# Narrow experts of a mixture of experts: left and right column products pinned in turns, and their middle columns turned by transpositions

## The chip, the core and the metric

One core of one Trainium2 chip runs the whole program once. The metric is the device time of that execution in microseconds (us), lower is better. Times are medians of the runs named.

## What is computed

A two-layer encoder on 256 tokens plus 16 learned ones, model width 1024, all float32. The change lies in the last part of layer 1, the top-2-of-8 SwiGLU experts with hidden width 3584:

```python
def swiglu(x, w_gate, w_up, w_down):
    return (jax.nn.silu(x @ w_gate) * (x @ w_up)) @ w_down

def moe_swiglu(x, w_router, b_router, w_gate, w_up, w_down):
    ...
    y = jnp.zeros(x.shape, jnp.float32)
    for e in range(N_EXPERTS):
        y = y + gates[..., e:e + 1] * swiglu(x, w_gate[e], w_up[e], w_down[e]).astype(jnp.float32)
    return y.astype(x.dtype)
```

Attention, the dense SwiGLU of layer 0, the RWKV mixer of layer 1 and the layer norms come before it or after it and are not touched.

## The kernel before

The experts are ordered by how many tokens chose them, and stand in the places `KINDS = 'WNWWNWWN'`. A wide place (W) has room for 128 tokens, a narrow one (N) for 64; there are five wide and three narrow ones. Each expert is worked in two tiles of `FT` = 1792 hidden columns, so the loop `for n in range(16)` in `moe` goes over 16 tiles. Tile n computes its gate and up products, while the hidden columns of tile n-1 are turned (put with the hidden index on the partitions) and multiplied with the down matrix. So three kinds of step share TensorE at any time: gate and up of this tile, turning of the last, down of the last. After an expert's second tile, `combine` (L1508, L1510) adds its result to the sum `ymoe`.

A wide tile takes every weight piece apart into two rounded halves, `w_hi` (ScalarE, L124) and `w_lo` (VectorE or GpSimd, L127), and makes three products of each (L1414 for gate and up, L134 to L136 for down). A narrow tile uses the raw float32 weights. Its 64 tokens fill only half of TensorE's 128 columns, so there are two products that stand beside each other: in `stream_narrow` (L1429) h = 0 is the gate product on the left 64 columns and h = 1 the up product on the right 64; in `down_narrow` (L1478) q = 0 and q = 1 are the left and right half of the output width. A float32 product shows as two records in the trace.

Turning is done in `hidden_narrow`: two steps for each tile, each of seven products with the identity (L1459, 64 rows by 128 strided hidden columns as the stationary operand, 64 identity columns moving), and a VectorE copy out of PSUM (L1460). `pt` and `hth` have one buffer each, so a step also waits for the copy before it. In wide tiles the same is done with transpositions (L1445). `hid`, the tile that is turned, is made by a SiLU on ScalarE (L1616) and a product on VectorE (L1618).

Weights come by SP's DMA queue (L1545), 896 KB each, into a ring of 17 buffers, in program order.

The order of instructions on each engine is not the order of the code: a scheduler sets it, by its own estimate of when each instruction is ready and by the dependences. `tc.keep_in_program_order(ins)` adds a dependence of issue order alone: `ins` comes behind the instruction that was traced just before it on its engine. Columns that an instruction uses, left or right, are part of the built program, not of the trace.

Of the kernel before, what the change touches and what calls it, by code (L numbers as in the profile page):

```python
# [17 lines left out]
NF = 8  # L18
# [8 lines left out]
FT = 1792  # L27
NB = FT // 128
# [66 lines left out]
class Trunk:  # L95
# [15 lines left out]
    def load(self, src, r0, kt, c0, nc_, pitch):  # L111

        raw = next(self.raws)()[:, :kt * nc_].rearrange("p (k c) -> p k c", k=kt)
        self.nc.sync.dma_start(raw, self.row_ap(src, r0 * pitch + c0, [[pitch, 128], [128 * pitch, kt], [1, nc_]]))
        return raw
# [1304 lines left out]
    def stream_narrow(self, psum, xs, load, steps):  # L1420

        ps = [psum.tile([128, 2, 512], F32, name="pgu", bufs=2) for _ in range(2)]
        for k in range(NF):
            raws = [load(kind, k) for kind in range(2)]
            for a in range(2):
                for b in range(2):
                    o = 896 * a + 448 * b
                    for h in range(2):
                        self.nc.tensor.matmul(ps[a][64 * h:64 * h + 64, b, :448], xs[:, k, :], raws[h][:, o:o + 448], start=k == 0,  # L1429
                                              stop=k == NF - 1)  # L1430
                for f in steps.pop(2 * k + a, ()):
                    f()
        return ps
# [17 lines left out]
    def hidden_narrow(self, mp, psum, s, H):  # L1451
        nc = self.nc

        def step(i0):
            if i0 == 0:
                H['h'] = mp.tile([128, NB, 64], F32, name="hth", bufs=1)
            pt = psum.tile([128, 7, 64], F32, name="pt", bufs=1)
            for j in range(7):
                nc.tensor.matmul(pt[:, j, :], s[64:128, i0 + j:FT:NB], self.ident[64:128, 64:128], start=True, stop=True)  # L1459
            nc.vector.tensor_copy(H['h'][:, i0:i0 + 7, :], pt)  # L1460

        return [lambda i=i: step(i) for i in (0, 7)]
# [11 lines left out]
    def down_narrow(self, h, load, pd, half, first, last):  # L1474
        for j in range(4 * half, 4 * half + 4):
            raw = load(j)
            for o, n, i, q, c in self.pieces(j, 0, FT):
                self.nc.tensor.matmul(pd[64 * q:64 * q + 64, c:c + n], h[:, i, :], raw[:, o:o + n], start=first and i == 0,  # L1478
                                      stop=last and i == NB - 1)

    @staticmethod
    def pieces(j, a, b):
# [253 lines left out]
```

## Time and profile before

| | us |
|---|---|
| median of 3 runs | 1922.72 (1917.08 to 1924.86) |
| the profiled execution, its own time | 1925.96 |
| its span, first to last instruction | 1923.9 |
| TensorE (PE) busy | 1764.4 (92%) |
| VectorE (DVE) busy | 1279.4 (66%) |
| ScalarE (ACT) busy | 913.4 (47%) |
| GpSimd (POOL) busy | 625.4 (33%) |
| mean granted TensorE clock | 0.934 of full speed |

Busy time is a union, so products that overlap are counted once. The experts take the stretch from about 900 us to 1906 us of the span; the first narrow tile's products start at 1000.7 us. The three narrow experts work at about 1000 to 1135, 1384 to 1515 and 1770 to 1900 us, with wide ones between. The granted clock has two levels, 2.4 GHz (1.00 in a stretch) and 1.2 GHz (0.50).

### The profile page before, as it was taken

The numbers are of one execution on the slowest core, as the hardware profiler recorded it, in microseconds if no ns is written. First come the engines' busy times: TensorE is split into PE (matmuls) and PEld (weight loads), VectorE is DVE, ScalarE is ACT, GpSimd is POOL, SyncE is SP. The second block draws the span as 40 slices with busy tenths as digits, with TensorE's granted clock in tenths as the row PEclk, the third lists the DMA queues.
The fourth block names the chain that finished last, engine by engine and source line by source line (L and its number), as shares of the span: only waits on it lengthen the run. The fifth ranks groups of instructions, "written<-read, shape, count | busy, mean of one in ns | idle before, by whom it ended". The sixth has DMA issues, their size and how long they took to land. (4 is left out here: it accounts for less than half of the span.)

```text
span 1923.9 us, 30672 instructions
## 1 busy us (share of the span) xinstructions
PE 1764.4 (92%) x11506; PEld 1406.3 (73%) x11506; DVE 1279.4 (66%) x2135; ACT 913.4 (47%) x1612; POOL 625.4 (33%) x551
## 2 busy tenths in 40 slices
PE   6997999978988878897999999999999999999995
PEld 6887999966666666777876577888765678887642
DVE  6886655587678786836884247999732478897412
ACT  4675444364254434434763135777531356765300
POOL 4333100256545544303542013544310134444201
PEclk9999999988788878888999999999999999999988
DMA  6331555521200000536699899989998999889980
GB/s 209 103 111 45 175 176 187 178 64 46 77 24 29 23 23 23 220 119 257 236 333 403 347 382 341 351 325 330 332 362 329 374 360 342 320 321 336 404 336 25
DMA packets 130737, 431.79 MB, mean 224 GB/s; under 512 B 13689, under 2 KB 78674, under 8 KB 130578
## 3 DMA queue, kind: packets, MB, share of 16 engines
q1 hardware_dynamic: 127202, 427.78, 60.4%
q10 hardware_dynamic: 3376, 1.95, 0.4%
q8 instruction: 92, 1.51, 0.3%
q14 instruction: 67, 0.55, 0.1%
HBM read 428.66 MB, written 1.05 MB: 223 GB/s over the span
## 5 line engine op out<-in xcount | busy, mean ns | idle before, releaser
L127 DVE TENSOR_TENSOR w_lo<-w_raw,w_hi 128x896 fp32r<-128x896 f32 (+2 forms) x445 | 648.9, 1498 | 163.0 <-ACT w_hi L124 159.1
L124 ACT CAST w_hi<-w_raw 128x896 fp32r<-128x896 f32 (+2 forms) x580 | 537.9, 960 | 271.6 <-PE pgu L1414 65.9
L127 POOL TENSOR_TENSOR w_lo<-w_raw,w_hi 128x1024 fp32r<-128x1024 f32 (+1 forms) x135 | 335.9, 2489 | 673.2 <-ACT w_hi L124 525.4
L1414 PE MATMUL pgu<-w_hi,xe 128*128 128x448 f32 x1280 | 305.2, 373 | 2.4 <-DVE hid L1610 1.6
L1414 PEld LDWEIGHTS pgu<-w_hi,xe 128*128 128x128 f32 x1280 | 240.2, 190 | 27.0 <-issue 5.1
L1429 PE MATMUL pgu<-w_raw,xs 128*64 128x448 f32 x768 | 173.7, 559 | 0.0
L1414 PE MATMUL pgu<-w_lo,xe 128*128 128x448 f32 x640 | 167.4, 371 | 5.4 <-DVE w_lo L127 5.3
L1414 PEld LDWEIGHTS pgu<-w_lo,xe 128*128 128x128 f32 x640 | 118.7, 189 | 22.4 <-DVE w_lo L127 8.9
L1429 PEld LDWEIGHTS pgu<-w_raw,xs 128*64 128x64 f32 x768 | 65.2, 140 | 87.6 <-issue 85.6
L135 PE MATMUL pd<-w_lo,hth 128*128 128x512 f32 (+1 forms) x320 | 121.7, 385 | 6.2 <-DVE w_lo L127 4.5
L136 PE MATMUL pd<-w_hi,htl 128*128 128x512 f32 (+1 forms) x320 | 119.5, 375 | 0.0
L134 PE MATMUL pd<-w_hi,hth 128*128 128x512 f32 (+1 forms) x320 | 100.4, 374 | 4.1 <-ACT w_hi L124 4.1
L1478 PE MATMUL pdn<-w_raw,hth 128*64 128x512 f32 (+1 forms) x384 | 85.5, 568 | 0.0
L135 PEld LDWEIGHTS pd<-w_lo,hth 128*128 128x128 f32 x320 | 62.0, 194 | 27.8 <-POOL w_lo L127 6.5
L134 PEld LDWEIGHTS pd<-w_hi,hth 128*128 128x128 f32 x320 | 58.5, 194 | 17.7 <-ACT w_hi L124 5.7
L134 PE MATMUL pj<-xh,w_hi 128*128 128x272 f32 x192 | 59.3, 309 | 11.7 <-ACT w_hi L124 4.7
L136 PEld LDWEIGHTS pd<-w_hi,htl 128*128 128x128 f32 x320 | 62.0, 194 | 9.1
L1478 PEld LDWEIGHTS pdn<-w_raw,hth 128*64 128x64 f32 x384 | 34.7, 143 | 39.5 <-issue 33.8
L136 PE MATMUL pj<-xh,w_lo 128*128 128x272 f32 x192 | 57.5, 300 | 0.6 <-DVE w_lo L127 0.6
L135 PE MATMUL pj<-xl,w_hi 128*128 128x272 f32 x192 | 57.3, 298 | 0.0
L1618 DVE TENSOR_TENSOR hid<-hid,pgu 64x896 f32<-64x896 f32 x12 | 12.9, 1091 | 61.1 <-ACT hid L1616 61.1
L139 DVE TENSOR_TENSOR htl<-pt,hth 128x512 fp32r<-128x512 f32 (+1 forms) x40 | 24.6, 616 | 41.3 <-ACT hth L139 41.3
(634 smaller groups left out, 3620.5 us busy)
## 6 DMA issues: line engine op xcount, KB each, us to landing
w_raw<-in_moe_w_down_dram SPq DMA_DIRECT2D x128, 896.0 KB, 7.1
w_raw<-in_moe_w_gate_dram SPq DMA_DIRECT2D x126, 896.0 KB, 7.0
w_raw<-in_moe_w_up_dram SPq DMA_DIRECT2D x126, 896.0 KB, 7.0
w_raw<-in_attn_w_in_dram SPq DMA_DIRECT2D x12, 1024.0 KB, 9.1
w_raw<-in_rw_w_rkv_dram SPq DMA_DIRECT2D x12, 1024.0 KB, 5.0
w_raw<-in_ffn_w_gate_dram SPq DMA_DIRECT2D x11, 1024.0 KB, 7.6
w_raw<-in_ffn_w_up_dram SPq DMA_DIRECT2D x11, 1024.0 KB, 5.1
w_raw<-in_ffn_w_down_dram SPq DMA_DIRECT2D x8, 1024.0 KB, 5.0
```

Of the source, the lines that this page charges most:

```text
L124: nc.scalar.copy(hi, raw)
L127: self.parted = eng.tensor_tensor(lo, raw, hi.bitcast(F32), op=OP.subtract)
L134: mm(ps, wh, xh, start=start, stop=False)
L135: mm(ps, wh, xl, start=False, stop=False)
L136: return mm(ps, wl, xh, start=False, stop=stop)
L139: return self.nc.scalar.copy(hi, src), (eng or self.nc.vector).tensor_tensor(lo, src, hi.bitcast(F32), op=OP.subtract)
L1414: mm(ps[a][:, b, :448], xe[:, x, k, :], w[:, 448 * b:448 * b + 448], start=k == 0 and i == 0, stop=k == NF - 1 and i == 2)
L1429: self.nc.tensor.matmul(ps[a][64 * h:64 * h + 64, b, :448], xs[:, k, :], raws[h][:, o:o + 448], start=k == 0, stop=k == NF - 1)
L1478: self.nc.tensor.matmul(pd[64 * q:64 * q + 64, c:c + n], h[:, i, :], raw[:, o:o + n], start=first and i == 0, stop=last and i == NB - 1)
L1618: nc.vector.tensor_tensor(cols(a)[64:128], cols(a)[64:128], pg[a][64:128, :, :448], op=OP.mult)
```

## The change

Three edits. The gate and up products of narrow tiles and their down products are pinned in program order, which is left, right, left, right. The turning products become transpositions: the same two operands, one pass in place of a float32 product.

```diff
@@ stream_narrow
                     for h in range(2):
-                        self.nc.tensor.matmul(ps[a][64 * h:64 * h + 64, b, :448], xs[:, k, :], raws[h][:, o:o + 448], start=k == 0,
-                                              stop=k == NF - 1)
+                        self.tc.keep_in_program_order(self.nc.tensor.matmul(
+                            ps[a][64 * h:64 * h + 64, b, :448], xs[:, k, :], raws[h][:, o:o + 448], start=k == 0, stop=k == NF - 1))
@@ hidden_narrow
             for j in range(7):
-                nc.tensor.matmul(pt[:, j, :], s[64:128, i0 + j:FT:NB], self.ident[64:128, 64:128], start=True, stop=True)
+                nc.tensor.transpose(pt[:, j, :], s[64:128, i0 + j:FT:NB], self.ident[64:128, 64:128])
@@ down_narrow
             for o, n, i, q, c in self.pieces(j, 0, FT):
-                self.nc.tensor.matmul(pd[64 * q:64 * q + 64, c:c + n], h[:, i, :], raw[:, o:o + n], start=first and i == 0,
-                                      stop=last and i == NB - 1)
+                self.tc.keep_in_program_order(self.nc.tensor.matmul(
+                    pd[64 * q:64 * q + 64, c:c + n], h[:, i, :], raw[:, o:o + n], start=first and i == 0, stop=last and i == NB - 1))
```

The scheduler's order changes with it. The first place is TensorE at the start of the second narrow expert (place 4), where its gate and up products (L1429) meet the down products of the wide tile before (L134 to L136), wide transpositions (L1445) and the gathering of the next expert's tokens (L1359).

```order
 L134 MATMUL pd_13078<-w_hi,hth 128x512
 L134 MATMUL pd_13079<-w_hi,hth 128x512
-L1429 MATMUL pgu<-w_raw,xs 64x448 x2
 L135 MATMUL pd_13078<-w_lo,hth 128x512
 L136 MATMUL pd_13078<-w_hi,htl 128x512
@@ -4403,5 +4376,5 @@
 L1429 MATMUL pgu<-w_raw,xs 64x448 x8
 L1445 MATMUL pt<-blob_61,hid 128x128 x4
-L1429 MATMUL pgu<-w_raw,xs 64x448 x6
+L1429 MATMUL pgu<-w_raw,xs 64x448 x8
 L1359 MATMUL pt<-og,h_9464 128x128 x8
 L1429 MATMUL pgu<-w_raw,xs 64x448 x8
```

The two narrow products that stood alone between wide ones (by the built program both on the left columns) are gone from there, and the run that had lost them has eight again.

The second place is TensorE a tile later, in the same expert's second tile: a turning step (L1459), the combination of the wide expert before (L1508) and gate and up products.

```order
 L1429 MATMUL pgu<-w_raw,xs 64x448 x8
-L1459 MATMUL pt<-blob_61,hid 128x64 x6
+L1459 MATMUL pt<-blob_61,hid 128x64 x7
 L1508 MATMUL pd_13814<-xe_13789,os 128x512 x2
-L1459 MATMUL pt<-blob_61,hid 128x64
 L1429 MATMUL pgu<-w_raw,xs 64x448 x8
 L1508 MATMUL pd_13830<-xe_13789,os 128x512 x2
-L1429 MATMUL pgu<-w_raw,xs 64x448 x8
+L1429 MATMUL pgu<-w_raw,xs 64x448
 L1508 MATMUL pd_13870<-xe_13855,os 128x512 x2
-L1429 MATMUL pgu<-w_raw,xs 64x448 x6
+L1429 MATMUL pgu<-w_raw,xs 64x448 x7
```

The turning step stays whole, and a run of eight products is now parted into one and seven. The list on SP, the order of the weight loads, is the same in both kernels.

Counted over the whole list by the columns of each product: an unbroken run of narrow products is one with no other TensorE instruction in it. Before there are 56 such runs; in their gate and up products, left and right counts differ by 40 in sum over the runs. After there are 45 runs, and the differences sum to 16. For the down products, the columns by which the longer half exceeds the mean are the same before and after. In the first narrow expert all products stand in turns; in the second and third, later products of a tile still stand in groups such as left, left, right, left, right, right, left, right. The turning steps are 15 runs of L1459 before and 13 after, 84 instructions in both.

## Rows read from the trace of the kernel before

**Rows 1.** The page: busy time by engine, and the granted clock in the 40 equal slices of the span (48.1 us each), in tenths of full speed.
```profile
PE 1764.4 (92%) x11506; PEld 1406.3 (73%) x11506; DVE 1279.4 (66%) x2135; ACT 913.4 (47%) x1612; POOL 625.4 (33%) x551
...
PEclk9999999988788878888999999999999999999988
```

**Rows 2.** Busy time in stretches of 20 us: stretch, its length, then busy us (and instructions) of PE, weight loads, DVE, ACT, POOL; granted clock, DMA share, GB/s. The third lies in a wide expert, the others in narrow ones.
```profile
1020.00:1040.00 20.00, 20.00 (x107) 9.08 (x104) 3.43 (x5) 1.17 (x2) 0.00 (x0) 1.00 1.01 414
...
1100.00:1120.00 20.00, 20.00 (x100) 13.68 (x96) 9.00 (x7) 7.19 (x8) 4.23 (x2) 1.00 1.02 425
...
1600.00:1620.00 20.00, 19.65 (x97) 17.87 (x98) 19.50 (x13) 14.79 (x17) 11.58 (x5) 1.00 0.94 339
...
1460.00:1480.00 20.00, 20.00 (x90) 8.21 (x90) 2.85 (x4) 0.59 (x1) 0.00 (x0) 0.93 0.81 317
```

**Rows 3.** The page's groups of the narrow products: busy us (union), mean ns of one record.
```profile
L1429 PE MATMUL pgu<-w_raw,xs 128*64 128x448 f32 x768 | 173.7, 559 | 0.0
...
L1478 PE MATMUL pdn<-w_raw,hth 128*64 128x512 f32 (+1 forms) x384 | 85.5, 568 | 0.0
```

**Rows 4.** The timeline of TensorE, records in order of time: start, length, line, operation, number of records (two for a narrow product). By the built program the run at 1060.48 is left and right in turns; the four records at 1383.83 are two products on the left; the run at 1386.60 is right, left, right, right, left, right, left, left.
```profile
1060.48 3.23 PE L1429 MATMUL pgu<-w_raw,xs 128*64 128x448 f32 x16
1063.64 0.72 PE L134 MATMUL pd<-w_hi,hth 128*128 128x512 f32 x2
...
1383.83 1.72 PE L1429 MATMUL pgu<-w_raw,xs 128*64 128x448 f32 x4
1385.48 0.50 PE L135 MATMUL pd<-w_lo,hth 128*128 128x512 f32 x1
...
1386.60 3.28 PE L1429 MATMUL pgu<-w_raw,xs 128*64 128x448 f32 x16
1389.81 2.05 PE L1359 MATMUL pt<-og,h 128*128 128x128 f32 x16
```

**Rows 5.** A turning step (L1459) and what follows it, in the timeline; then the two nearest kinds of transposition: L1445 (128 rows, hidden columns with the same stride, 128 identity columns) in a wide tile, and L864 (64 rows, not strided, 64 identity columns) in the RWKV part. The last two rows are each line's minimum, median and maximum ns.
```profile
1068.71 3.61 PE L1459 MATMUL pt<-blob,hid 64*128 64x64 f32 x14
1072.26 3.98 PE L1429 MATMUL pgu<-w_raw,xs 128*64 128x448 f32 x20
...
1033.21 0.73 PE L1445 MATMUL pt<-blob,hid 128*128 128x128 f32 x4
1033.87 5.47 PE L1429 MATMUL pgu<-w_raw,xs 128*64 128x448 f32 x26
...
1046.04 0.62 PE L1445 MATMUL pt<-blob,hid 128*128 128x128 f32 x4
...
570.37 0.47 PE L864 MATMUL pa<-blob,BK 64*128 64x64 f32 x8
...
L864 PE MATMUL pa<-blob,BK x128: 221/223/366, 491.9 to 796.0; 64*128 64x64 f32 x128
...
L1445 PE MATMUL pt<-blob,hid x140: 270/279/383, 948.0 to 1781.9; 128*128 128x128 f32 x140
```

**Rows 6.** The eleven stretches from 1000 to 1900 us in which the granted clock was at its lower level; columns as in rows 2, and the sum of all eleven. They begin at 1083.7, 1121.3, 1131.5, 1425.1, 1455.8, 1489.9, 1507.0, 1698.1, 1804.0, 1838.1 and 1868.8 us; all but the one at 1698.1 begin within 6 us after a step of L1459 began. Of the twelve steps, those that begin at 1068.7 and 1884.5 us are followed by none. The last row is the stretch between the third and the fourth.
```profile
1083.70:1087.20 3.50, 3.50 (x11) 1.31 (x12) 1.35 (x2) 0.59 (x1) 0.00 (x0) 0.51 0.17 72
...
1455.80:1462.60 6.80, 6.80 (x19) 3.17 (x21) 1.29 (x2) 0.00 (x0) 0.00 (x0) 0.50 0.43 171
...
1698.10:1701.60 3.50, 3.50 (x11) 2.76 (x10) 2.61 (x3) 0.83 (x1) 0.00 (x0) 0.51 0.54 158
...
1868.80:1875.60 6.80, 6.80 (x21) 3.03 (x22) 0.00 (x0) 0.00 (x0) 0.00 (x0) 0.50 0.96 401
sum 51.20, PE 51.20 PEld 33.80 DVE 18.05 ACT 7.45 POOL 4.05; mean PE 4.65 PEld 3.07 DVE 1.64 ACT 0.68 POOL 0.37
...
1134.90:1420.00 285.10, 276.46 (x1376) 218.99 (x1374) 217.72 (x169) 167.85 (x201) 104.48 (x43) 1.00 0.92 337
```

**Rows 7.** The timeline of TensorE in and after the low stretch from 1455.8 to 1462.6 us: two runs of eight products with the same order of halves, and what follows each.
```profile
1458.23 5.41 PE L1429 MATMUL pgu<-w_raw,xs 128*64 128x448 f32 x16
1463.58 0.73 PE L1508 MATMUL pd<-xe,os 128*128 128x512 f32 x2
1464.24 3.28 PE L1429 MATMUL pgu<-w_raw,xs 128*64 128x448 f32 x16
1467.45 0.73 PE L1508 MATMUL pd<-xe,os 128*128 128x512 f32 x2
```

**Rows 8.** The weight loads: the page's row of one kind (KB each, us to landing), the issue of the first down weights of the first narrow expert, their first use, and the longest wait of SP's queue from 930 to 1900 us (total us, times, longest).
```profile
w_raw<-in_moe_w_down_dram SPq DMA_DIRECT2D x128, 896.0 KB, 7.1
...
1062.64 0.33 SPq L1545 DMA_DIRECT2D w_raw<-in_moe_w_down_dram  x1
...
1100.40 0.59 PE L1478 MATMUL pdn<-w_raw,hth 128*64 128x512 f32 x1
...
SPq L1545 <- DVE w_lo L127: 519.4, 216, 7.4
```

**Rows 9.** Wide pieces: VectorE's part of taking weights apart from 1000 to 1900 us (busy us, mean ns of one), one piece at 1104.10 us, and two wide down products in the timeline.
```profile
L127 DVE TENSOR_TENSOR w_lo<-w_raw,w_hi 128x896 fp32r<-128x896 f32 (+2 forms) x305 | 459.6, 1554 | 92.7 <-ACT w_hi L124 90.2 <-PE pgu L1414 2.4
...
1104.10 2.26 DVE L127 TENSOR_TENSOR w_lo<-w_raw,w_hi 128x896 fp32r<-128x896 f32 x1 [0.71 <-ACT w_hi L124]
...
1044.64 0.39 PE L134 MATMUL pd<-w_hi,hth 128*128 128x512 f32 x1
1044.88 0.39 PE L135 MATMUL pd<-w_lo,hth 128*128 128x512 f32 x1
```

## The prediction

> **What bounds the kernel now.** First the page: TensorE is busy for 92% of the span, no other engine for more than 66% [rows 1]. That is an average, so next the stretches. In narrow experts TensorE is busy for all 20.00 us of 20 while VectorE works 2.9 to 9.0 us and ScalarE 0.6 to 7.2 [rows 2]. In a wide expert both are near full (19.65 and 19.50 us of 20). So a saving of TensorE time in a narrow expert shortens the kernel as long as the weights keep up; in a wide one it would not.
>
> The weights keep up with room. A first down load of a narrow expert is issued at 1062.64 us, such a load lands after 7.1, and it is first used at 1100.40 [rows 8]: some 30 us to spare. SP's queue waits mostly for a free buffer (519.4 us on VectorE alone), so the ring sets the lead and not the DMA.
>
> How much could narrow products give? The timeline prices them [rows 4]. Eight products in turns take 3.16 us from their start to the next instruction's (1060.48 to 1063.64), two on one half take 1.65 (1383.83 to 1385.48). If a pair, left beside right, costs p and a run a fixed f, then 4p + f = 3.16 and 2p + f = 1.65, since two products on one half cannot share: p = 0.755, f = 0.14. I use 0.75 and 0.16, which also gives 3.16. Each product without a partner in its run thus costs half a pair, 0.375 us, more than its share. Out of turn alone costs next to nothing: the run right, left, right, right, left, right, left, left takes 3.21 us (1386.60 to 1389.81). So what counts is whether left and right balance within a run, not their strict turn.
>
> The 384 gate and up products (768 records) would take 192 x 0.75 = 144 us if all had partners at full clock; the 192 down products, mostly of 512 columns, half as much, 72. Their rows say 173.7 and 85.5 us, 259 together [rows 3]. So 43 us are lost there to missing partners, run starts and low clock: a ceiling for the first edit and the clock together.
>
> **Pinning.** By the order of the built programs, left and right gate and up products differ by 40 in sum over the runs before and by 16 after: (40 - 16) x 0.375 = 9.0 us. Down products keep their imbalance. Runs go from 56 to 45, 11 x 0.16 = 1.8 us. Together 10.8 us. Nothing is added on any other engine; SP's order is the same. Later in a tile the second and third expert still have products out of turn, which costs little [rows 4].
>
> What stands behind a pinned product? Everything later on TensorE, as before, but now a narrow product can no longer be moved ahead into a wait of the wide down products for `w_lo`. There should be few such waits: a wide down tile has 16 pieces, of which VectorE takes about three quarters, 12 x 1.554 = 18.6 us [rows 9], against TensorE's 84 products' worth (28 of 512 columns, three times) at 0.24 us = 20.2. It is close, and I charge 5 us for the three places and for the hand-over from narrow to wide together, an estimate.
>
> **Transpositions.** There are 84 of these products in twelve steps of seven. A step takes 3.55 us now (1068.71 to 1072.26, 14 records, 0.25 us a record) [rows 5]. A transposition is one record, so the dearest case is 7 x 0.25 = 1.8 us, a saving of 1.75 a step, 21 us in all. The cheapest is L864, the same form without the stride: eight in 0.47 us, so 0.5 a step, a saving of 3.05, 36.6 us. L1445 has the same stride of the hidden columns and twice the identity columns: four take 0.66 us until the next instruction starts (1033.21 to 1033.87), and each more takes (0.62 - 0.28) / 3 = 0.113, with 0.62 from the row at 1046.04 and 0.28 the median. Seven take 0.66 + 3 x 0.113 = 1.00 us. I take this one, since the stride is what could slow the weight load: a saving of 2.55 a step, 12 x 2.55 = 30.6 us. All steps lie where TensorE is full or on the chain at the end. The VectorE copy behind a step (L1460) stays.
>
> **The clock.** Eleven stretches of the expert part, 51.2 us, are at 1.2 GHz; ten of them, 47.7 us, follow one of the twelve turning steps within 6 us, and in the 285 us from 1134.9 on, which hold no such step, there is none [rows 6]. So the long steps of small products bring the clock down, and the products after them pay. How much: eight products take 5.35 us (1458.23 to 1463.58) against 3.21 for the same order a moment later (1464.24 to 1467.45) [rows 7]. The 2.14 us are 63% of half of that stretch (3.4 us); the rest of it passed under the step itself, which is counted already. So 47.7 / 2 x 0.63 = 15 us, at most 20, return if steps of 1 us no longer bring the clock down. That a short group of transpositions leaves it alone is shown by L1445, which runs inside the 285 us at full clock.
>
> The Trainium skill says otherwise of transpositions (TensorE: Matmul & The Clock Gate, Part 4: PE-mode transpose): they do not count as TensorE activity for the clock. By this rule the drops could stay although the steps are shorter, and the sum would be without these 15 us. The trace has groups of four at a time in wide tiles, and no drop behind them, so it does not bear the rule out for short groups; groups of seven in a narrow tile no run before shows.
>
> **The sum.** 30.6 + 10.8 + 15 - 5 = 51.4 us off the profiled execution's own 1925.96 gives 1874.6. That execution is 3.2 us above the median of the runs, 1922.72; off the median it is 1871.3, and I say 1871.
>
> **Rivals.**
> *The clock still falls.* The ten low stretches stay, by the page's rule or because narrow products themselves keep activity low. For it: the low stretch at 1698.1 has no turning step before it. Against it: a full clock in the narrow stretch from 1020 to 1040 us [rows 2]. Then 30.6 + 10.8 - 5 = 36.4, so 1886.
> *A transposition costs as much per record as the product did*, because the strided load of 64 rows sets the pace and not the pass. Then 21 + 10.8 + 15 - 5 = 41.8, so 1881.
> *The weights become the bound.* A tile of the second kind in a narrow expert has 24 loads of 0.917 MB, 22 MB, 52 us at the 425 GB/s of the fullest row [rows 2], while TensorE would need about 24 for gate and up, 12 for down, 2 for turning and 4 for combining, 42. The load falls 10 us behind once in each narrow expert, out of 30 us to spare; it decides only if the lead were under 10. If it does, about 10 us for each of the three experts are given back, 30 us: 1901. If only the later half suffers, 1890.
> *Slower: wide down products starve.* Pinned behind them, narrow products no longer fill the holes. If each of the 16 pieces took VectorE 2.26 us, as one does while GpSimd works too [rows 9], a tile would take 36 us instead of 20, a loss of 16 at three places, 48: the gain of 56 would shrink to 8, 1915. It ends above 1922 from 2.5 us a piece on. The mean of 1.554 speaks against it.
> *It changes nothing.* If transposition were carried out in two passes like the product and the runs lost elsewhere what they gain, the time would stay near 1920; the one record of L864 and L1445 for each instruction speaks against it.
>
> **The numbers.** The forecast, 1858 to 1884 by its own bounds (36.6 and 20 at the good end, some further loss at the other), gets 0.60; the clock that still falls 0.14; dear transpositions 0.07; weights as the bound 0.10; starving or no change 0.09, half of it slower. The range from 1852 to 1897 leaves out the last and part of the weights' case. A measurement of this kernel tells a change from none from about 0.5%, 9.6 us. Faster 0.91, within 0.5% 0.05, slower 0.04.
>
> **What would show it.** L1459 with 84 records in place of 168 and steps of about 1.0 us instead of 3.6; L1429 busy for about 155 us and L1478 for about 80; no stretch of low clock behind the turning steps; the mean clock above 0.934; TensorE still busy for 20 of 20 us in narrow stretches; time from first to last narrow product shorter by some 15 us in each narrow expert, and the wide ones between as long as before. It is wrong if L1459's records lie 0.2 us or more apart, if the low stretches return at the same places, or if TensorE or ScalarE waits for `w_raw`.

## The result, and the profile after

The changed kernel takes 1870.8 us in the median of 4 runs (1868.09 to 1873.26), the kernel before 1921.26 on the same chip; the ratio is 0.9725, 95% interval 0.9704 to 0.9747. The forecast was 1871. The profiled execution took 1868.09 us with a span of 1866.0, against 1925.96 and 1923.9 before.

Of the page of the changed kernel, the lines that answer to [rows 1] and [rows 3]: busy time, the granted clock by slices, and the two groups of narrow products.

```profile
PE 1704.3 (91%) x11422; PEld 1362.5 (73%) x11422; DVE 1275.7 (68%) x2135; ACT 912.2 (49%) x1612; POOL 624.8 (33%) x551
...
PEclk9999999988878878897999999999999999999998
...
L1429 PE MATMUL pgu<-w_raw,xs 128*64 128x448 f32 x768 | 158.1, 544 | 0.0
...
L1478 PE MATMUL pdn<-w_raw,hth 128*64 128x512 f32 (+1 forms) x384 | 79.6, 542 | 0.0
```

TensorE lost 60 us of busy time and 84 records; the other engines did what they did before. L1429 fell by 15.6 us and L1478 by 5.9.

A turning step in the timeline of TensorE (answers to [rows 5]), and its line's minimum, median and maximum:

```profile
1068.60 1.02 PE L1459 MATMUL pt<-blob,hid 64*128 64x64 f32 x7
1069.55 0.97 PE L1429 MATMUL pgu<-w_raw,xs 128*64 128x448 f32 x4
```
```profile
L1459 PE MATMUL pt<-blob,hid x84: 275/277/374, 1055.4 to 1829.9; 64*128 64x64 f32 x84
```

Seven records instead of fourteen, and 0.95 us to the start of the next instruction instead of 3.55.

Next the expert part, from the first expert's first gate product (L1414) to the start of the last narrow expert's last down product (L1478), before and after (stretch, length, busy us and instructions of PE, PEld, DVE, ACT, POOL; granted clock, DMA share, GB/s):

```profile
897.70:1899.70 1002.00, 973.71 (x4656) 723.63 (x4655) 642.37 (x512) 492.20 (x581) 302.82 (x125) 0.97 0.88 332
```
```profile
893.90:1841.80 947.90, 915.27 (x4572) 681.68 (x4571) 640.12 (x512) 491.28 (x581) 302.01 (x125) 0.99 0.92 351
```

54.1 us went from this part. The same work now has the DMA busy for 0.92 of the time instead of 0.88. TensorE's idle time there grew, from 28.3 us (1002.00 - 973.71) to 32.6. The part ahead of the experts was 3.8 us shorter in this execution (893.9 against 897.7 us); in two further profiled executions of the changed kernel it took 888.9 and 891.5, so it varies by as much by itself. Parted at the narrow experts (a narrow part ends where that expert's last product of L1478 starts, a wide one where the next narrow expert's first gate product does):

| us | to the end of narrow expert 1 | wide between | narrow expert 2 | wide between | narrow expert 3 | sum |
|---|---|---|---|---|---|---|
| before | 284.6 | 201.5 | 182.3 | 203.5 | 130.1 | 1002.0 |
| changed | 265.2 | 204.5 | 162.2 | 202.9 | 113.0 | 947.9 |
| transpositions alone | 271.1 | 203.6 | 167.5 | 202.0 | 117.0 | 961.2 |
| pinning alone | 277.9 | 202.9 | 176.9 | 204.5 | 126.3 | 988.5 |

The three parts with the narrow experts gave 17 to 20 us each; the first wide part lost 3.0 us, the second gave 0.6. The two further executions of the changed kernel gave 947.8 and 947.9, so differences of 1 us in this table can be read.

The low clock (answers to [rows 6]): the only stretches at 1.2 GHz in the expert part of the changed kernel, columns as above.

```profile
1291.60:1295.00 3.40, 3.40 (x10) 2.62 (x9) 2.21 (x3) 1.23 (x2) 0.00 (x0) 0.50 0.55 173
1400.80:1407.70 6.90, 6.27 (x18) 5.21 (x19) 4.77 (x4) 2.73 (x4) 2.95 (x2) 0.51 1.02 426
1759.20:1766.10 6.90, 6.24 (x24) 5.05 (x23) 4.55 (x4) 3.75 (x5) 3.57 (x2) 0.51 1.01 423
```

Eleven stretches have become three. But two of 6.9 us are still at a turning step, the first one of narrow experts 2 and 3. What TensorE did ahead of them is in its timeline, with the wait and what ended it in brackets; the first rows are of the changed kernel at both places, the others of the kernel before at the same two:

```profile
1398.98 0.74 PE L134 MATMUL pd<-w_hi,hth 128*128 128x512 f32 x2 [2.07 <-ACT w_hi L124]
1399.64 1.02 PE L1459 MATMUL pt<-blob,hid 64*128 64x64 f32 x7
...
1401.43 0.79 PE L135 MATMUL pd<-w_lo,hth 128*128 128x512 f32 x1 [0.76 <-POOL w_lo L127]
...
1758.71 0.80 PE L134 MATMUL pd<-w_hi,hth 128*128 128x512 f32 x2 [2.07 <-ACT w_hi L124]
1759.44 1.07 PE L1459 MATMUL pt<-blob,hid 64*128 64x64 f32 x7
```
```profile
1421.95 0.73 PE L134 MATMUL pd<-w_hi,hth 128*128 128x512 f32 x2 [2.07 <-ACT w_hi L124]
1422.61 3.66 PE L1459 MATMUL pt<-blob,hid 64*128 64x64 f32 x14
...
1802.44 0.72 PE L134 MATMUL pd<-w_hi,hth 128*128 128x512 f32 x2 [2.07 <-ACT w_hi L124]
```

These two stretches stood behind a wait of 2.07 us before the change too (they began at 1425.1 and 1804.0), and the third, at 1291.6, stands 0.7 us behind a wait of 2.09 us, as the one at 1698.1 of before did behind one of 2.07. So eight of the ten low stretches that the prediction put down to turning steps went, and the two that also had a wait of 2 us in front stayed. At narrow expert 3 the low stretch (from 1759.2) even begins before the turning step does (1759.44), so this step did not bring it on; in the second execution it is 1754.0 against 1754.54. A wait of that length does not always have a low stretch behind it. The changed kernel has four of 2.07 to 2.09 us in the expert part, and behind this one the clock stayed at its upper level, in all three executions:

```profile
1657.59 0.39 PE L135 MATMUL pd<-w_lo,hth 128*128 128x256 f32 x1 [2.09 <-DVE w_lo L127]
```

The 0.76 us at L135 is new: the float32 step had covered it.

Where that wait comes from shows in ScalarE's timeline of the changed kernel:

```profile
1395.44 0.91 ACT L1616 ACTIVATE hid<-pgu 64x896 f32<-64x896 f32 x1 [10.29 <-PE pgu L1429]
1396.95 0.91 ACT L1616 ACTIVATE hid<-pgu 64x896 f32<-64x896 f32 x1 [0.60 <-PE pgu L1429]
```

ScalarE's list has the two SiLUs ahead of the next casts of the wide down weights (L124). It waits 10.29 us for the gate products, and TensorE, when these are done, for the casts.

The loads (answers to [rows 8]): the stretch after the first narrow expert, and ScalarE's waits for loads from 995 to 1850 us (total us, times, longest); the last row is the only such wait of the kernel before, from 995 to 1905 us.

```profile
1100.00:1120.00 20.00, 20.00 (x113) 17.50 (x110) 15.97 (x13) 10.67 (x13) 7.28 (x3) 1.00 1.02 426
```
```profile
ACT w_hi L124 <- DMA w_raw<-in_moe_w_down_dram: 5.8, 2, 3.0
ACT w_hi L124 <- DMA w_raw<-in_moe_w_gate_dram: 4.7, 2, 4.4
```
```profile
ACT w_hi L124 <- DMA w_raw<-in_moe_w_down_dram: 5.9, 1, 5.9
```

The DMA is full around the narrow experts, and ScalarE waits 10.5 us for it, 4.6 more than before the change. These waits lie at 1010, 1014, 1093 and 1095 us, where TensorE has narrow products to do, and none of its waits there follows. Whether the loads hold it back by another way is asked below.

### The profile page after: what moved, and what is told of

The parts are those of the page before. It is cut to its first block, busy times and chain, and to the rows that moved or that the text cites. A ratio compares the mean times of both kernels' runs of the same rounds, so it can differ in the third digit from the quotient of the medians.

```text
span 1866.0 us, 30513 instructions
## 1 busy us (share of the span) xinstructions
PE 1704.3 (91%) x11422; PEld 1362.5 (73%) x11422; DVE 1275.7 (68%) x2135; ACT 912.2 (49%) x1612; POOL 624.8 (33%) x551
## 4 chain that ended last, share of the span: by engine, by line
PE 36%; issue 5%; DVE 4%; DMA 3%; POOL 1%; ACT 1%; SPq 0%; DVEq 0%; POOLq 0%; ACTq 0%
PE pgu L1414 14%; PE pgu L1429 6%; PE pd L135 3%; PE pdn L1478 3%; PE pd L136 3%; PE pd L134 3%; DVE w_lo L127 2%; DMA w_raw<-in_moe_w_down_dram 1%; POOL w_lo L127 1%; DMA w_raw<-in_moe_w_up_dram 1%; DMA w_raw<-in_moe_w_gate_dram 1%; DVE hid L1610 1%; PE pd L1508 1%; PE pt L1359 1%; PE pt L1445 1%
## 5 line engine op out<-in xcount | busy, mean ns | idle before, releaser
L124 ACT CAST w_hi<-w_raw 128x896 fp32r<-128x896 f32 (+2 forms) x580 | 537.2, 960 | 277.1 <-PE pd L136 70.9
L1414 PE MATMUL pgu<-w_hi,xe 128*128 128x448 f32 x1280 | 299.6, 369 | 2.4 <-DVE hid L1610 1.6
L1414 PEld LDWEIGHTS pgu<-w_hi,xe 128*128 128x128 f32 x1280 | 237.4, 188 | 26.7 <-issue 6.5
L1414 PE MATMUL pgu<-w_lo,xe 128*128 128x448 f32 x640 | 164.5, 369 | 4.7 <-DVE w_lo L127 4.6
L1429 PE MATMUL pgu<-w_raw,xs 128*64 128x448 f32 x768 | 158.1, 544 | 0.0
L1414 PEld LDWEIGHTS pgu<-w_lo,xe 128*128 128x128 f32 x640 | 118.5, 188 | 18.9 <-DVE w_lo L127 8.1
L135 PE MATMUL pd<-w_lo,hth 128*128 128x512 f32 (+1 forms) x320 | 121.3, 384 | 10.0 <-DVE w_lo L127 6.3
L136 PE MATMUL pd<-w_hi,htl 128*128 128x512 f32 (+1 forms) x320 | 119.7, 375 | 0.0
L1429 PEld LDWEIGHTS pgu<-w_raw,xs 128*64 128x64 f32 x768 | 59.1, 136 | 81.0 <-issue 76.9
L134 PE MATMUL pd<-w_hi,hth 128*128 128x512 f32 (+1 forms) x320 | 101.3, 376 | 4.1 <-ACT w_hi L124 4.1
L135 PEld LDWEIGHTS pd<-w_lo,hth 128*128 128x128 f32 x320 | 62.3, 195 | 28.9 <-DVE w_lo L127 8.3
L1478 PE MATMUL pdn<-w_raw,hth 128*64 128x512 f32 (+1 forms) x384 | 79.6, 542 | 0.0
L134 PEld LDWEIGHTS pd<-w_hi,hth 128*128 128x128 f32 x320 | 58.9, 194 | 17.3 <-ACT w_hi L124 5.7
L136 PEld LDWEIGHTS pd<-w_hi,htl 128*128 128x128 f32 x320 | 62.1, 194 | 10.2 <-issue 0.7
L134 PE MATMUL pj<-xh,w_hi 128*128 128x272 f32 x192 | 58.5, 305 | 9.8 <-ACT w_hi L124 4.9
L1478 PEld LDWEIGHTS pdn<-w_raw,hth 128*64 128x64 f32 x384 | 32.5, 137 | 37.8 <-issue 30.4
L136 PE MATMUL pj<-xh,w_lo 128*128 128x272 f32 x192 | 56.7, 295 | 0.6 <-DVE w_lo L127 0.6
L135 PE MATMUL pj<-xl,w_hi 128*128 128x272 f32 x192 | 56.5, 294 | 0.0
```

The costliest lines, as they stand in the source:

```text
L124: nc.scalar.copy(hi, raw)
L134: mm(ps, wh, xh, start=start, stop=False)
L135: mm(ps, wh, xl, start=False, stop=False)
L136: return mm(ps, wl, xh, start=False, stop=stop)
L1414: mm(ps[a][:, b, :448], xe[:, x, k, :], w[:, 448 * b:448 * b + 448], start=k == 0 and i == 0, stop=k == NF - 1 and i == 2)
L1429: self.tc.keep_in_program_order(self.nc.tensor.matmul(ps[a][64 * h:64 * h + 64, b, :448], xs[:, k, :], raws[h][:, o:o + 448], start=k == 0 ...
```

## Experiments

Every kernel was run against the kernel before on its chip; ratios have the 95% interval.

**1. Each edit alone.** `x1_turn_only` has the transpositions without any pinning, `x2_pin_only` the pinning with the float32 turning products:

```diff
@@ x1_turn_only, against the changed kernel (L1429 and L1478)
-self.tc.keep_in_program_order(self.nc.tensor.matmul(...))
+self.nc.tensor.matmul(...)
@@ x2_pin_only, against the changed kernel (L1459)
-nc.tensor.transpose(pt[:, j, :], s[64:128, i0 + j:FT:NB], self.ident[64:128, 64:128])
+nc.tensor.matmul(pt[:, j, :], s[64:128, i0 + j:FT:NB], self.ident[64:128, 64:128], start=True, stop=True)
```

> The turning products are transpositions, nothing is pinned. Theory A (the terms of the prediction add up): steps of 1.0 us save 12 x 2.55 = 30.6, the clock gives back about 15, and since the built order of this kernel has 2.4 us more of missing partners than the kernel before (20.3 against 17.9 us) that is lost: 43 off 1921, so 1878, with the low stretches behind the turning steps gone. Rival B (most of the gain is the pinning): nearer to 1900 than to 1878.

> Both kinds of narrow products are pinned, the turning products stay float32 products. Theory A: missing partners fall from 17.9 to 11.2 us by the built order and runs from 56 to 47 (9 x 0.16 = 1.4): 8 off 1921, so 1913, and some ten low stretches of the clock behind the turning steps as before. Rival B: nearer to 1890.

Measured: transpositions alone 1878.21 us, ratio 0.9766 (0.9735 to 0.9797); pinning alone 1906.58, ratio 0.9913 (0.9884 to 0.9942). In the table above they take 40.8 and 13.5 us from the expert part, together 54.3 where both edits at once take 54.1. The narrow products in the two pages, transpositions alone first:

```profile
L1429 PE MATMUL pgu<-w_raw,xs 128*64 128x448 f32 x768 | 169.9, 545 | 0.0
```
```profile
L1429 PE MATMUL pgu<-w_raw,xs 128*64 128x448 f32 x768 | 163.1, 547 | 0.0
```

With transpositions alone the same three low stretches are left as in the changed kernel. So the step from it to the changed kernel is pinning at one and the same clock: L1429 169.9 to 158.1 and L1478 82.4 to 79.6, 14.6 us. With pinning alone seven low stretches, 37.5 us, are left in the expert part, where the kernel before has eleven with 51.2 us; four of the seven, 20.4 us, follow a turning step with no wait of 1 us or more in front of it. So this kernel is 6 us faster than expected, and its 13.5 us are in part a gain of clock: L1429 and L1478 give 9.7 us, less than the 14.6 behind the transpositions, and the wide products (L1414) give 5.9 (418.36 to 412.49 us), where behind the transpositions they give 1.6. That the two edits add up to 0.2 us is therefore partly luck: what pinning alone gains by the clock, the transpositions gain too.

**2. The down products not pinned.** `x3_pin_gate_up` takes `keep_in_program_order` off L1478 alone.

```diff
@@ x3_pin_gate_up (L1478)
-self.tc.keep_in_program_order(self.nc.tensor.matmul(...))
+self.nc.tensor.matmul(...)
```

> The changed kernel with the down products not pinned. Theory A (the gain of pinning is the balance of gate and up products; pinning down products adds nothing): missing partners 10.2 us against 9.0 and 49 runs against 45, so 2 slower than the changed kernel, no difference that can be told. Rival E (down products in turns are worth as much as gate and up products): 5 or more slower.

Measured 1868.84 us, ratio 0.9706 (0.9681 to 0.9732); the changed kernel on the same chip (`x0_changed_again`) took 1864.59, ratio 0.9688 (0.9647 to 0.9729), some 6 us less than in the result above and than expected. The intervals overlap: this third of the change can't be told from nothing by time. L1478 is 81.6 us instead of 79.6, so its size is about 2 us.

> The changed kernel once more, beside the three that follow on the same chip: 1871 to 1875, ratio to the kernel before 0.97.

**3. Does turn matter, or balance alone?** `x4_llrr` pins left, left, right, right, and `x5_llll` four left, then four right; `x5_llll` also hands in the steps that stand between the products after eight of them and not after four. In the code left and right balance in every eight products; in the built order the expectations count 7 and 9 us more of missing partners than in the changed kernel.

```diff
@@ x4_llrr (stream_narrow)
-                for b in range(2):
-                    o = 896 * a + 448 * b
-                    for h in range(2):
+                for h in range(2):
+                    for b in range(2):
+                        o = 896 * a + 448 * b
@@ x5_llll (stream_narrow)
-            for a in range(2):
-                for b in range(2):
-                    o = 896 * a + 448 * b
-                    for h in range(2):
+            for h in range(2):
+                for a in range(2):
+                    for b in range(2):
+                        o = 896 * a + 448 * b
...
+            for a in range(2):
                 for f in steps.pop(2 * k + a, ()):
```

> The changed kernel, but the code issues left, left, right, right within a run (gate of both column blocks, then up of both), pinned in that order. Theory A (only the balance of left and right within a run counts, not the strict turn): by the built order 15.7 us of missing partners against 9.0, so 7 slower than the changed kernel, 1878. Rival C (each neighbour on the same half costs 0.375 us by itself): 242 such neighbours against 51, 72 us slower, 1942.

> The changed kernel with its gate and up products pinned in another turn: four on the left half, then four on the right. Within every run left and right still balance as well as before the change or better (differences 40 in sum over the runs, 16 in the changed kernel). Theory of balance alone, as the prediction has it: (40 - 16) x 0.375 = 9 us more than the changed kernel, about 1878. Theory of a short look-ahead (the kernel that issues two and two showed that left, left, left, left, right, right, right, right takes 4.71 us where turns take 3.16, and 24 products in such groups 13.09, 4.36 for eight): 48 groups of eight at 1.2 to 1.55 us more each, 58 to 74 us, so 1927 to 1943, slower than the kernel before; L1429 busy for 215 to 230 us instead of 158.

Measured: 1885.45 us, ratio 0.9794 (0.9759 to 0.9830), and 1917.97 us, ratio 0.9986 (0.9957 to 1.0014). So `x5_llll` gives the whole gain away: 54 us more than the changed kernel on the same chip (1863.96). Neither expectation of balance alone held. The first four rows are from the timeline of `x4_llrr`, the others from that of `x5_llll`; all four runs are at full clock and, by the built programs, in groups of four.

```profile
1371.44 4.78 PE L1429 MATMUL pgu<-w_raw,xs 128*64 128x448 f32 x16
1376.15 0.73 PE L1445 MATMUL pt<-blob,hid 128*128 128x128 f32 x4
...
1395.97 11.02 PE L1429 MATMUL pgu<-w_raw,xs 128*64 128x448 f32 x48
1409.06 1.05 PE L134 MATMUL pd<-w_hi,hth 128*128 128x512 f32 x2 [2.07 <-ACT w_hi L124]
```
```profile
1014.62 4.78 PE L1429 MATMUL pgu<-w_raw,xs 128*64 128x448 f32 x16
1019.33 0.50 PE L134 MATMUL pd<-w_hi,hth 128*128 128x512 f32 x1
...
1063.50 7.90 PE L1429 MATMUL pgu<-w_raw,xs 128*64 128x448 f32 x32
1071.33 0.73 PE L1509 MATMUL pd<-xe,os 128*128 128x512 f32 x2
```

Eight products as four left and four right take 4.71 us where turns take 3.16, though the run is balanced. Groups of two take 3.21 (eleven such runs in `x4_llrr`), nearly as turns. Sixteen in groups of four take 7.83, only 3.12 more than eight. So the second half starts about two products late, and the lag of 1.55 us is paid about once in each run, not once for each eight, as the expectation for `x5_llll` had it. Its 13.09 us for 24 products are those from 1395.97 to 1409.06 in `x4_llrr`, and they end in a wait of 2.07 us for a cast; the products themselves take 11.02 us. So it was at least 9 us too high, and L1429 is busy for 206.2 us, not 215 to 230. In `x4_llrr` the scheduler made groups of four out of some groups of two (30 groups by the built program); L1429 is busy for 177.0 us there, and the expert part is 16.4 us longer than the changed kernel's, not 7.

**4. Is it the kind of instruction or the length of the step that brings the clock down?** `x6_turn4` issues each narrow transposition four times over; the result is the same.

```diff
@@ x6_turn4 (hidden_narrow)
-                nc.tensor.transpose(pt[:, j, :], s[64:128, i0 + j:FT:NB], self.ident[64:128, 64:128])
+                for _ in range(4):
+                    nc.tensor.transpose(pt[:, j, :], s[64:128, i0 + j:FT:NB], self.ident[64:128, 64:128])
```

> The changed kernel with each transposition issued four times into the same place. A step has 28 transpositions and takes 0.95 + 21 x 0.11 = 3.3 us, about as long as the float32 steps before: 12 x 2.4 = 28 us slower by itself, and 3 more of missing partners in the built order. Theory A (it was the length of the step with little work in the array that brought the clock down, whatever the kind): the low stretches come back behind most of the twelve steps, about 15 us more, 1871 + 46 = 1917. Rival D (transpositions leave the clock alone, only the float32 products of 64 columns brought it down): no low stretches, 1902.

Measured 1911.49 us, ratio 0.9934 (0.9909 to 0.9959). A whole step in the timeline (L1460 is this kernel's line of the transposition), and the low stretch behind it:

```profile
1122.85 3.46 PE L1460 MATMUL pt<-blob,hid 64*128 64x64 f32 x28
1126.24 1.30 PE L1414 MATMUL pgu<-w_hi,xe 128*128 128x448 f32 x4
```
```profile
1126.90:1130.30 3.40, 3.40 (x11) 3.01 (x10) 1.16 (x2) 1.38 (x2) 0.00 (x0) 0.50 1.01 424
```

A step of 28 takes 3.39 us, like one of float32 products, and the low stretches are back behind it: eight in the expert part instead of three, five of them with no wait of 1 us or more in front. The expert part is 40.2 us longer than the changed kernel's, of which the steps explain 12 x (3.39 - 0.95) = 29; the total lies between the two expectations, and the low stretches decide for the first. So transpositions that fill 3.4 us bring the clock down as float32 products do, and ten of the twelve steps of 0.95 us in the changed kernel do not (the other two stand behind a wait). The rule of the Trainium skill that the prediction weighed (TensorE: Matmul & The Clock Gate, Part 4: PE-mode transpose) agrees with this run, which does not prove it, since float32 products in steps of that length did the same. With steps as short as the change makes them it did not decide the time.

**5. Do the loads hold the changed kernel back?** `x7_gate_twice` loads no up weights in narrow tiles (it leaves the up product out and uses the gate weights twice), a third less to load there. `x9_more_loads` does the reverse: 98 KB more with each gate and up load, into a buffer of its own.

```diff
@@ x7_gate_twice (stream_narrow)
-            raws = [load(kind, k) for kind in range(2)]
+            raws = [load(0, k)] * 2
@@ x9_more_loads (load)
                 nc.sync.dma_start(raw.unsqueeze(1), views[kind][:, at, o])
+                if narrow:
+                    extra = mp.tile([128, 192], F32, name="extra", bufs=2)
+                    nc.sync.dma_start(extra.unsqueeze(1), views[kind][:, at, <first 192 columns of o>])
```

> The changed kernel, but a narrow tile loads no up weights and uses the gate weights in their place (the up product is left out of the result that way), so each narrow tile loads 14.7 MB and not 22. The built order of this kernel has no missing partners (0.0 against 9.0 us) and 41 runs against 45, which is 9.6 us by itself. Theory A (weights that fall behind in the first narrow expert cost next to nothing): 10 faster than the changed kernel. Rival F (the loads, which run at 426 GB/s without a break from 1060 to 1200 us in the changed kernel, hold the wide tiles behind the first narrow expert up): 14 or more faster, most of the excess between 1100 and 1360 us.

> The changed kernel; beside each of the 32 gate and up loads of a narrow expert SP also loads 98 KB of the same weights into a spare buffer that nobody reads: 3.1 MB in each narrow expert, 7.4 us of DMA time at 425 GB/s, 22 us in the three. TensorE's order stays nearly the same (left and right differ by 20 in sum over the runs instead of 16, 1.5 us). Theory that the loads do not hold the changed kernel back (no wait of TensorE in it ends on a load, and the lead of 12 to 16 us covers 7.4): 1 to 5 us above the changed kernel, 1866 to 1875. Theory that they do, since the DMA is full from 1060 to 1200 us and the kernel that loads a third less was 29 us faster: most of the 22 us come on top, 1882 to 1890, with ScalarE or TensorE waiting for w_raw in the narrow experts.

Measured: 1835.79 us, ratio 0.9540 (0.9515 to 0.9566), and 1881.30, ratio 0.9799 (0.9774 to 0.9825). By the totals both speak for the loads as a bound: 29 us less and 17 us more than the changed kernel on the same chip (1864.59 and 1863.96). The traces say otherwise. First the expert part of `x7_gate_twice`:

```profile
890.90:1810.00 919.10, 898.74 (x4572) 672.81 (x4571) 638.36 (x512) 498.81 (x581) 292.94 (x125) 1.00 0.85 315
```

Of its 28.8 us, 9.6 come from L1429 and L1478 (152.3 and 75.8 us on its page), as balance alone had it, since no run is unbalanced there. TensorE's idle time falls from 32.6 to 20.4 us, 12.2, and the low clock from 17.2 us to 3.4, at most half of 13.8, 6.9. The idle time that is gone is the 2.07 us waits for casts and the like, and none of these ended on a load in the changed kernel. The scheduler, which plans with the loads, had chosen another order on every engine. So this run tested another order as well as fewer loads, and can't part the two.

In `x9_more_loads` the order on TensorE stayed nearly the same. Its parts are 265.4, 204.5, 163.6, 204.5 and 125.9 us: narrow experts 1 and 2 took some 7.4 us more of loading each (an estimate: 3.1 MB at 425 GB/s) with 0.2 and 1.4 us more time, the wide part behind them 1.6 more (a low stretch at 1655.4), and expert 3 lost 12.9. SP's queue in that expert in the timeline of `x9_more_loads`, with a stretch of 20 us, the queue's longest wait there (total us, times, longest) and TensorE's first wait behind it; the last two rows are the queue of the changed kernel in its third execution:

```profile
1770.40 0.33 SPq L1545 DMA_DIRECT2D w_raw<-in_moe_w_up_dram  x1
1796.24 0.34 SPq L1180 DMA_DIRECT2D xe<-in_ln_g_dram  x1
```
```profile
1780.00:1800.00 20.00, 19.45 (x91) 8.56 (x91) 5.45 (x8) 1.17 (x2) 0.00 (x0) 1.00 0.08 33
```
```profile
SPq L1180 <- DVE xe L139: 20.9, 1, 20.9
```
```profile
1804.42 0.97 PE L1429 MATMUL pgu<-w_raw,xs 128*64 128x448 f32 x2 [2.00 <-DMA w_raw<-in_moe_w_gate_dram]
```
```profile
1778.53 15.64 SPq L1545 DMA_DIRECT2D w_raw<-in_moe_w_down_dram  x7
1796.80 0.34 SPq L1180 DMA_DIRECT2D xe<-in_ln_g_dram  x1
```

The two small loads of the last layer norm (L1180) need a buffer that comes free only at 1796 us. In the changed kernel 9 weight loads stand behind them; in `x9_more_loads` 22 do, and the DMA was idle for 20 us (share 0.08) with weights still to fetch. TensorE then waits for weights, 5.8 us in sum, and the clock is low from 1805.6 to 1812.4 us; the changed kernel has neither there. That stall, and not the transfer time of the added bytes, made it slower. The number is just below the expectation of the loads as a bound, and the cause is another. What stands: in experts 1 and 2 hardly any of the added 7.4 us came through.

**6. Removing the wait in front of the low stretches.** `x8_down_early` traces the first half of the wide down products ahead of a narrow tile's last gate and up products, so that their casts come ahead of the SiLU.

```diff
@@ x8_down_early (moe, narrow tile)
+                    early = prev and KINDS[prev[0]] == 'W'
+                    if early:
+                        one.setdefault(11, []).append(lambda: down(prev[0], prev[1], H['h'], 0))
...
-                    for half in range(2):
+                    for half in range(1 if early else 0, 2):
```

> The changed kernel; in a narrow tile that follows a wide one the first half of the wide down products is traced before the last gate and up products and not behind them. In the changed kernel ScalarE's casts of the wide down weights stand behind the SiLU of the narrow tile, TensorE waits 3 to 4 us at the second and third narrow expert, and the two low stretches of the clock that are left (6.9 us each) lie there. Theory A (waits and a short turning step together bring the clock down; without the waits it stays up): both low stretches go, 2 x (3.5 + 2.2) = 11 faster, less 1.5 of missing partners and 0.6 for runs (10.5 us against 9.0, 49 against 45): 1862. Rival G (the turning step is what brings it down there too): the low stretches stay, 1866.

Measured 1869.01 us, ratio 0.9720 (0.9691 to 0.9748): not faster than the changed kernel. TensorE's timeline at narrow expert 2:

```profile
1403.84 0.74 PE L134 MATMUL pd<-w_hi,hth 128*128 128x512 f32 x2 [0.57 <-ACT w_hi L124]
1406.27 0.50 PE L135 MATMUL pd<-w_lo,hth 128*128 128x512 f32 x1 [1.70 <-POOL w_lo L127]
...
1412.54 0.79 PE L135 MATMUL pd<-w_lo,hth 128*128 128x512 f32 x1 [1.34 <-DVE w_lo L127]
```

The waits of the changed kernel, 2.07 and 0.76 us (2.8 together, not 3 to 4 as expected), became others: the one for the cast shrank to 0.57 us, and TensorE waited instead for the other half of the pieces, `w_lo`, 1.70 and 1.34 us; a low stretch of 3.4 us begins in the second of these waits, and at expert 3 one of 6.8 as before. This kernel doesn't show what the place would cost without a wait. `x7_gate_twice` has such places, in its own order on TensorE: the first turning steps of narrow experts 2 and 3 (1400.95 and 1737.74 us) have no wait in front, and the clock stays up. The step, and the stretch around it:

```profile
1400.39 0.63 PE L134 MATMUL pd<-w_hi,hth 128*128 128x512 f32 x2
1400.95 1.02 PE L1459 MATMUL pt<-blob,hid 64*128 64x64 f32 x7
```
```profile
1394.70:1407.70 13.00, 13.00 (x67) 9.41 (x63) 9.34 (x9) 6.28 (x8) 2.40 (x1) 1.00 0.87 345
```

So a step of 0.95 us alone does not bring the clock down there.

**7. The rest of the balance.** `x10_pin_steps` pins L1459 and L1508 too, so that they part no run at an odd place.

```diff
@@ x10_pin_steps (hidden_narrow, combine)
-                nc.tensor.transpose(pt[:, j, :], ...)
+                self.tc.keep_in_program_order(nc.tensor.transpose(pt[:, j, :], ...))
-                nc.tensor.matmul(ps, os, x, start=i == 0, stop=i == len(Y[q]) - 1)
+                self.tc.keep_in_program_order(nc.tensor.matmul(ps, os, x, start=i == 0, stop=i == len(Y[q]) - 1))
```

> The changed kernel; the narrow turning transpositions (L1459) and the products of the combination (L1508) are pinned in program order too, so that they stand between groups of four gate and up products and no longer part a run at an odd place. By the built program, the differences of left and right sum to 6 over the runs instead of 16, with 47 runs instead of 45. Theory of balance: (16 - 6) x 0.375 - 2 x 0.16 = 3.4 us faster than the changed kernel, about 1865 against 1868, if nothing waits for it. Rival: a pinned step stands in front of products that could go ahead, and the wait for hid, for the copy out of PSUM or for the combination's buffer holds TensorE: one to two us at each of some 18 steps, so up to 20 us slower, with new waits at L1459 or L1508.

> The changed kernel once more, to stand beside the other kernels of this call on one chip: 1864 to 1872, as in its other runs.

Measured 1863.23 us, ratio 0.9704 (0.9676 to 0.9731), beside 1863.96, ratio 0.9707 (0.9679 to 0.9735), of the changed kernel on the same chip: no difference. L1429 and L1478 fell by 5.3 us, to 155.1 and 77.3, more than the 3.4 expected. But the wide parts took 206.9 and 208.6 us instead of 204.5 and 202.9, and with the other parts the expert part is 949.7 instead of 947.9. The new waits, from 890 to 1850 us (the last row is that of the changed kernel for the first):

```profile
PE pgu L1414 <- DVE w_lo L127: 8.5, 12, 1.1
...
PE pt L1445 <- DVE htl L139: 4.3, 3, 1.9
```
```profile
PE pgu L1414 <- DVE w_lo L127: 4.6, 6, 1.0
```

The gain went into waits of wide tiles. Its five low stretches say something more: none lies behind a turning step, and four of the five begin 0.7 to 1.9 us behind a wait of TensorE of 1.7 to 2.1 us. Two of them are at the places of the two stretches of 6.9 us of the changed kernel. The first, with what is ahead of it:

```profile
1397.12 0.74 PE L134 MATMUL pd<-w_hi,hth 128*128 128x512 f32 x2 [2.07 <-ACT w_hi L124]
1399.56 0.50 PE L135 MATMUL pd<-w_lo,hth 128*128 128x512 f32 x1 [1.71 <-POOL w_lo L127]
```
```profile
1400.40:1403.80 3.40, 3.40 (x13) 2.91 (x12) 1.93 (x2) 1.88 (x2) 1.61 (x1) 0.51 1.02 428
```

Here the wait is and the turning step is not (it comes at 1425.2), and the clock falls all the same, for half as long.

## Why the prediction was right, step by step

- **What bounds it.** Right: the narrow experts gave 19.4, 20.1 and 17.1 us in the parts of the table that hold them, the wide parts together cost 2.4.
- **Transpositions, 30.6 us.** Right. L1459 has 84 records, a step takes 0.95 us where 1.00 was worked out from L1445: 12 x 2.60 = 31.2. The strided wide transposition was the right neighbour; by L864, without the stride, it would have been 0.5. The rival of dear records is out: seven records take 0.95 us, not 1.8.
- **Pinning, 10.8 us.** Right in kind, a little too small. At one clock it gave 14.6 (experiment 1), 11.8 of it in L1429 and 2.8 in L1478. But that is measured from transpositions alone, whose built order has 2.4 us more of missing partners than the kernel before (20.3 against 17.9, by its expectation at the prediction's price). Against the kernel before, pinning is then worth 14.6 - 2.4 = 12.2, and the cause of the last 1.4 us stays open. "What counts is whether left and right balance within a run" does not hold for four in a row on one half (experiment 3), but that is not the cause: by the built programs neither the kernel before, nor transpositions alone, nor the changed kernel has more than two in a row.
- **The clock, 15 us.** Right in size by two errors that offset. Ten stretches were put down to turning steps by nearness alone; the two at 1425.1 and 1804.0 also had a wait of 2.07 us in front, and they stayed: 34.1 of 47.7 us went. By the prediction's rate that would be 10.7. With transpositions alone, L1429 and L1478 fell by 6.9, though their order was 2.4 worse, so 9.3 came from the clock; the wide products (L1414) fell from 418.36 to 413.19 us in the expert part, 5.2. With L1508 and L1359 (0.9 and 0.7) that is 16.1. So the rate of 63% was too low: it was read off the stretch at 1455.8, part of which lay over its step, and L1459 fills only 3.0 of the 34.1 us that went; half of the other 31.1 is 15.5. That the length of the step matters is shown by experiment 4. The two stretches left at turning steps don't need the step: one begins before it, the same steps without a wait leave the clock up (experiment 6), and the clock falls where the wait stands without the step (experiment 7). That the wait alone brings them on is not shown, since a like wait at 1657.59 has none behind it and these kernels differ in order; nor is it shown why they last 6.9 us with the step and 3.4 without.
- **Give-back, 5 us.** Right in size: TensorE's idle time in the expert part rose by 4.3 us. The reason is only in part the one that was charged, pinned products that can no longer fill holes: with transpositions alone and nothing pinned it already rose by 2.2 us (961.20 - 930.75 = 30.45 us). Part of it are waits that the long step had covered, such as the 0.76 us at 1401.43.
- **The sum.** 31.2 + 12.2 + 16.1 - 4.3 = 55.2, against 54.1 in the expert part (busy times overlap a little). The forecast's 51.4 lay 3 to 4 us below. That 1871 met 1870.8 so closely is luck: on two other chips the changed kernel took 1864.59 and 1863.96.
- **The rivals.** The clock that still falls: no, but for two stretches. Weights as the bound: the DMA is full where the prediction feared, and its sign, a wait for `w_raw`, is there on ScalarE; but the kernel before has that sign too (5.9 us), so it tells nothing. Narrow experts 1 and 2 took some 7.4 us more of loading with hardly any loss, so the loads held nothing back there. For expert 3 experiment 5 doesn't settle it, since the stall covered it; in the changed kernel no wait of TensorE there ends on a load. Wide down products that starve: the waits for `w_lo` and `w_hi` grew by single us, not by 16 a place.

## What to carry to other kernels

Price an instruction that the trace does not have by the nearest one with the same access (here the stride), and count a long group of tiny operations twice, for its own time and for the clock behind it. Before a slow stretch is put down to the operation beside it, look for what else stands in front of it, above all a wait: what has two causes doesn't go with one. And a run that changes a total as a rival says has not confirmed it until the trace shows the place: an edit of loads can reorder a scheduler's lists, and an in-order queue can stall on a small transfer.

## What the hardware showed beyond that

Products on the two halves of TensorE's columns run beside each other in turns and in twos, and not fully in fours: eight take 3.16 us in turns, 3.21 in twos, 4.71 in fours, and the lag of about 1.55 us is paid about once a run (three in a row were not run). And the granted clock fell to 1.2 GHz behind 3.4 us of transpositions with 64 identity columns as it did behind as long a step of float32 products. Single steps of 0.95 us with no wait of 2 us in front left it at 2.4 GHz in the changed kernel and, with one exception, in `x7_gate_twice`, where two such steps at 1793.90 and 1795.64 us with a wait of 0.72 us between them have a low stretch of 3.4 us behind them.
